# RWKV stage of a two-layer trunk: the state products in one PSUM bank, the other bank for the centred values and the first of each pair of chunk products, and new places for all pieces

## The chip, the core and the metric

One core of a Trainium2 chip runs the whole program. Its engines are named PE (TensorE), ACT (ScalarE), DVE (VectorE), POOL (GpSimd) and SP (SyncE, which issues the DMAs). The metric is the device time of one launch in microseconds (us).

## The reference, cut to what matters

Two layers on 2048 tokens of width 1024, each wrapped in RMS norms. Layer 0 is gated linear attention, layer 1 is RWKV-7 time mixing. The change is in the second one, whose recurrence per head is:

```python
p = h @ w_in
p = p + mu * (token_shift(p) - p)
r, k, v, gate, wd, ad = jnp.split(p, [...])
...
def step(S, inp):
    r_t, w_t, k_t, v_t, kk_t, a_t = inp
    sa = jnp.einsum('bhvk,bhk->bhv', S, -kk_t)
    S = (S * w_t[:, :, None, :] + sa[..., None] * (kk_t * a_t)[:, :, None, :]
         + v_t[..., None] * k_t[:, :, None, :])
    y = jnp.einsum('bhvk,bhk->bhv', S, r_t)
    return S, y
...
y = ((y - mean) * lax.rsqrt(var + GN_EPS)).reshape(B, T, RWKV_WIDTH)
...
y = y * jax.nn.silu(gate)
return y.astype(h.dtype) @ w_out
```

## The kernel before

The kernel runs the linear attention first (until about 890 us), then its output projection mixed with the start of the RWKV layer, then 32 RWKV steps (one step is one pair of heads and 512 tokens; `step`), and the last output projection. An RWKV step is cut into about 150 named pieces: a piece is a few instructions of one engine. The table `PLACE` gives every piece a number. Step n puts a piece at time n plus that number, and one heap hands all pieces of all steps out in the order of these times, under a manual schedule for PE, DVE, ACT and POOL. So the table alone decides what stands behind what on each engine, and pieces with numbers 2.x of one step stand between pieces 0.x of the step two later. The projections of the coming step are the filler: a piece `f` or `e` issues six 128x512 matmuls into a bank `ps_pj` (sixteen such pieces in most steps, twenty in each eighth).

PSUM has eight banks, given out by tag: `PB` says how many banks a tag has, and a tile takes the next one of its tag in turn, waiting until the last reader of that bank is done. Before: pj 2, tp 2, x 1, ch 2, y 1.

The pieces that the texts speak of, in the order in which one step needs them:

- `pn`, `n_ln`, `n_exp`, `unit`, `ra_a`, `bk_b`: the key's norm (PE, ACT, ACT, DVE, DVE, DVE).
- `pA` (L1361): products of all chunks, for four chunks at a time, two banks (one for each head); `mask` (DVE, L1370) and `diag` (ACT, L1380, reads the masked tile into `AD`) follow.
- `pB`, `tokens` (ACT, L1397): chunk keys turned. `elim` (28 DVE pieces, L1422 and L1425), `spread` (DVE, L1436 and L1438), `inv_t`, then `pL`, `pM`, `pW`, `pT` (PE, bank x) with `wt`, `Ti`, `Tl` between them (ACT, L1495, L1501, L1516): the triangular inverse.
- `pv` and `ve`: the values times a centring matrix. `pv` fills one bank in two halves, `pv0` and `pv1`, and `ve0` and `ve1` (ACT, L1325, four copies each) read them out, the first half before `pv1` is issued.
- `X` (ACT, L1527 and L1528), `pX` (PE, bank x), `Z` (ACT, L1544), `turn` (PE, L1564), `turned` (ACT, L1568), `pG` (PE), `G` (DVE, L1583): the chunk maps; `pG0` and `pG1` of the texts are the maps of the first and the last four chunks (two pieces each).
- `pS`, `next_state` (ACT, L1604): eight chunk states in a chain, each one matmul and two ACT instructions.
- `py` (bank y), `y_copy` (ACT, L1618), `y_high`, `y_sq` (ACT, L1628, L1623), `y_low` (DVE, L1633), `pg` (PE), `g_ln`, `g_exp` (ACT, L1642, L1646): the output and its norm. `pw` and `pa` are the products of the decay and the rate, `s_exp` (ACT, L1177) reads `pw`.

PE rows have line L103 (the helper `mm`) and are known by their tiles. What the change touches of the allocation:

```python
T.pv = self.ps("tp", [P, NC_ // 2, 2, C])
...
T.pA[cg] = [self.ps("tp", [P, 4, 2 * C]) for _ in range(2)]
...
T.pG[cg] = [self.ps("tp", [P, 4, 2 * C]) for _ in range(2)]
...
T.pS[c] = self.ps("ch", [P, 2, C])
...
T.pg = self.ps("ch", [P, TB])
```

## Time and profile before

| what | value |
|---|---|
| time, median of 3 runs | 2500.66 us (2500.08 to 2507.4) |
| profiled execution: its own time | 2500.48 us |
| profiled execution: span of the trace | 2498.4 us |
| busy PE / weight loads / ACT / DVE / POOL | 2404.0 / 2011.4 / 1646.3 / 1601.1 / 1065.7 us |
| the same, share of the span | 96% / 81% / 66% / 64% / 43% |
| PE idle before its instructions, 1050 to 2300 us, largest | 18.1 us behind `ve` |

A launch takes 2.08 us more than the span of its trace. The busy time of PE is modelled at the ends of its matmuls, so 96% doesn't say how much of it could go; that is read from the idle time ahead of single instructions, which stands in square brackets in a timeline, with what ended it.

### The profile page before, as it was taken

The page shows a single profiled execution, that of the slowest core. Times are in us where ns is not written, and L with a number is a line of the kernel's source. Part 1 is how long each engine was busy: PE and PEld are TensorE (multiplying, and loading weights), DVE is VectorE, ACT ScalarE, POOL GpSimd, SP SyncE. Part 2 cuts the span into 40 slices and gives each one's busy share as a digit, 9 for nine tenths or more (in the row PEclk, how much of TensorE's full clock was granted, in tenths as well). Part 3 has the DMA queues.
Part 4 walks back from the last instruction along what each step waited for, and adds up shares of the span by engine and source line. Part 5 has one row for each costly group of instructions (what it writes and reads, how often), then busy time and mean ns, then how long its engine had stood idle before and what let it go on. Part 6 is the DMA issues. An engine that isn't in the chain of part 4 may idle for free.

```text
span 2498.4 us, 53047 instructions
## 1 busy us (share of the span) xinstructions
PE 2404.0 (96%) x20049; PEld 2011.4 (81%) x20049; DVE 1601.1 (64%) x3339; ACT 1646.3 (66%) x3890; POOL 1065.7 (43%) x1557
## 2 busy tenths in 40 slices
PE   7999999999999998989999999999999999998998
PEld 6988888898878877767878788778788777887777
DVE  6544676346743368887777776777767787776432
ACT  6534565434533356876888988888888889886531
POOL 3213423123456556766543434334343434343442
PEclk9999999999999999998999999999999999999999
DMA  4211333113546565444433333333333333323482
GB/s 148 81 57 51 110 114 104 43 60 95 165 149 223 162 221 176 145 141 138 150 113 132 125 118 114 109 120 125 124 110 114 113 123 123 120 88 111 149 256 93
DMA packets 251863, 312.85 MB, mean 125 GB/s; under 512 B 18746, under 2 KB 180185, under 8 KB 251609
## 3 DMA queue, kind: packets, MB, share of 16 engines
q1 hardware_dynamic: 251608, 309.47, 37.4%
q8 instruction: 159, 2.61, 0.4%
q14 instruction: 96, 0.78, 0.1%
HBM read 230.77 MB, written 78.64 MB: 124 GB/s over the span
## 4 chain that ended last, share of the span: by engine, by line
PE 37%; ACT 18%; DVE 4%; issue 2%; DMA 1%; POOL 1%; POOLq 0%; SPq 0%; ACTq 0%; DVEq 0%
PE ps_pj L103 20%; PE ps_tp L103 9%; PE ps_x L103 3%; ACT AD L1380 2%; PE ps_ch L103 2%; ACT ve L1604 2%; ACT ts L836 1%; ACT ve L1325 1%; PE ps_y L103 1%; ACT BK L1397 1%; ACT y L1618 1%; PE ps_tp L1564 1%; ACT wt L1495 1%; ACT sq L1278 1%; DVE pp L1422 1%
## 5 line engine op out<-in xcount | busy, mean ns | idle before, releaser
L103 PE MATMUL ps_pj<-R,wh 128*128 128x512 f32 x3648 | 1172.8, 402 | 3.8 <-ACT wh L139 1.0
L103 PEld LDWEIGHTS ps_pj<-R,wh 128*128 128x128 f32 x3648 | 656.5, 190 | 131.0 <-issue 3.4
L103 PE MATMUL ps_pj<-R,wl 128*128 128x512 f32 x1824 | 718.2, 394 | 1.1 <-POOL wl L994 1.1
L103 PEld LDWEIGHTS ps_pj<-R,wl 128*128 128x128 f32 x1824 | 343.8, 188 | 79.8 <-POOL wl L994 1.9
L1604 ACT ACTIVATE ve<-ps_ch,cs 64x64 f32<-64x64 f32 x448 | 137.8, 308 | 61.3 <-PE ps_ch L103 52.5
L1422 DVE TENSOR_TENSOR pp<-L 128x14 f32<-128x14 f32 (+6 forms) x448 | 168.1, 375 | 10.5
L103 PE MATMUL ps_tp<-R,wh 128*128 128x512 f32 x512 | 158.3, 390 | 2.1 <-DVE ts L400 1.7
L1425 DVE TENSOR_TENSOR L<-L,pp 128x14 f32<-128x14 f32 (+6 forms) x448 | 139.9, 312 | 12.2
L832 POOL TENSOR_SCALAR carr<-ts 128x1 f32<-128x1 f32 x132 | 34.2, 259 | 241.1 <-ACT ts L836 240.8
L1551 POOL TENSOR_SCALAR A<-ra 64x512 f32<-64x512 f32 x128 | 90.0, 703 | 103.4 <-PE ps_x L103 51.9
L308 POOL TENSOR_TENSOR s<-s,cc 128x1 f32<-128x1 f32 (+1 forms) x96 | 57.6, 602 | 150.7 <-DVE s L306 138.4
L103 PE MATMUL ps_ch<-ve,BK 128*128 128x128 f32 x512 | 109.5, 296 | 7.8 <-ACT ve L1604 7.5
L103 PEld LDWEIGHTS ps_tp<-R,wh 128*128 128x128 f32 x512 | 95.8, 188 | 22.8 <-issue 2.5
L103 PEld LDWEIGHTS ps_ch<-ve,BK 128*128 128x128 f32 x512 | 87.1, 189 | 30.9 <-ACT ve L1604 11.4
L1380 ACT COPY AD<-A 32x128 f32<-32x128 f32 x256 | 105.1, 411 | 10.2 <-DVE A L1370 7.2
L836 ACT ACTIVATE ts<-ps_pj,prm 128x512 f32<-128x512 f32 x132 | 91.4, 692 | 18.7 <-PE ps_pj L103 10.7
L1370 DVE TENSOR_TENSOR A<-ps_tp,mask 128x512 f32<-128x512 f32 x128 | 82.3, 683 | 32.6 <-PE ps_tp L103 32.6
L103 PE MATMUL ps_tp<-R,wl 128*128 128x512 f32 x256 | 99.7, 390 | 0.0
L1583 DVE TENSOR_TENSOR BK<-ps_tp,BK 128x256 f32<-128x256 f32 x128 | 53.7, 419 | 69.6 <-PE ps_tp L103 69.6
L103 PE MATMUL ps_pj<-wh,R 128*128 128x256 f32 (+1 forms) x500 | 94.7, 287 | 0.0
L103 PE MATMUL ps_ch<-wh,R 128*128 128x256 f32 (+1 forms) x500 | 94.3, 286 | 0.0
L798 POOL TENSOR_SCALAR y<-BK,cs 128x256 f32<-128x256 f32 x64 | 36.6, 571 | 132.4 <-DVE BK L800 121.3
(358 smaller groups left out, 5518.3 us busy)
## 6 DMA issues: line engine op xcount, KB each, us to landing
wh<-w SPq DMA_DIRECT2D x99, 512.0 KB
wl<-w SPq DMA_DIRECT2D x99, 512.0 KB
w<-wh SPq DMA_DIRECT2D x33, 512.0 KB
w<-wl SPq DMA_DIRECT2D x33, 512.0 KB
Ti<-in_gla_w_in_dram SPq DMA_DIRECT2D x32, 512.0 KB
ws<-in_gla_w_in_dram SPq DMA_DIRECT2D x32, 512.0 KB
...
```

Source lines behind the costliest of these rows:

```text
L103: return self.nc.tensor.matmul(out, lhsT, rhs, start=start, stop=stop)
L308: nc.gpsimd.tensor_tensor(r[:, 0:w], u[:, 0:w], self.nhalf.broadcast_to([P, w]), op=ALU.pow)
L798: nc.gpsimd.tensor_scalar(Qf[:, n % 2, :], Qn, f[:, n:n + 1], 0.0, op0=ALU.mult, op1=ALU.add)
L832: self.put(name + ".carry", lambda: nc.gpsimd.tensor_scalar(cr, ts[:, TB:TB + 1], 1.0, 0.0, op0=ALU.mult, op1=ALU.add))
L836: nc.scalar.activation(ts[:, 1:TB + 1], pp, AF.Copy, scale=self.v["mu"][:, blk:blk + 1])
L1370: dve.tensor_mul(T.A[cg][:, :, :, h, :], V(T.pA[cg][h]), V(self.mask.unsqueeze(1).broadcast_to([P, 4, 2 * C])))
L1380: act.copy(T.AD[q, :, :, cg * 4:cg * 4 + 4].rearrange("p t u c -> p c u t"), T.A[cg][q, :, 0, h, 32 * b:32 * b + 32].rearrange("p c (u t) ...
L1422: dve.tensor_mul(T.u, T.M[:, s + 1:16, s:s + 1].broadcast_to([P, m, s]), T.M[:, s:s + 1, 0:s].broadcast_to([P, m, s]))
L1425: dve.tensor_add(T.M[:, s + 1:16, 0:s], T.M[:, s + 1:16, 0:s], T.u)
L1551: pool.tensor_scalar(T.A[cg][H[h], :, :, h, :], T.ra[H[h], cg * 4:cg * 4 + 4, :].rearrange("p c (b t) -> p c b t", b=2), 1.0, 0.0, op0=ALU ...
L1583: dve.tensor_add(o, T.pG[cg][h][:, :, x], o)
L1604: act.activation(o, x, AF.Copy, scale=k)
```

## The change

The tag ch goes from two banks to one, and a new tag tv gets the bank. In the linear attention and in the output projections the two tiles that took ch in turn now name ch and tv, one each. In an RWKV step `pS` and `pg` share the one bank ch; `pv` moves from tp to tv; of each pair of `pA` and of `pG` the first moves to tv and the second stays in tp. All numbers of `PLACE` are new (two lines of the table are shown).

```diff
-    PB = dict(pj=2, tp=2, x=1, ch=2, y=1)
+    PB = dict(pj=2, tp=2, x=1, ch=1, tv=1, y=1)
...
-                tp = self.ps("ch", [P, 4, P])
+                tp = self.ps(("ch", "tv")[ch], [P, 4, P])
...
-            pv = [self.ps(t, [P, w]) for t in ("ch", "ch", "pj", "pj")]
+            pv = [self.ps(t, [P, w]) for t in ("ch", "tv", "pj", "pj")]
...
-        ("pick", (0.773633, 0.800002)), ("pn", 0.286577), ("pv", (0.805045, 0.854518)), ("pw", 0.000000),
...
+        ("pick", (0.737006, 0.854736)), ("pn", 0.283275), ("pv", (0.740546, 0.872544)), ("pw", 0.000000),
...
-                T.pv = self.ps("tp", [P, NC_ // 2, 2, C])
+                T.pv = self.ps("tv", [P, NC_ // 2, 2, C])
...
-                T.pA[cg] = [self.ps("tp", [P, 4, 2 * C]) for _ in range(2)]
+                T.pA[cg] = [self.ps(t, [P, 4, 2 * C]) for t in ("tv", "tp")]
...
-                T.pG[cg] = [self.ps("tp", [P, 4, 2 * C]) for _ in range(2)]
+                T.pG[cg] = [self.ps(t, [P, 4, 2 * C]) for t in ("tv", "tp")]
```

Outside the RWKV steps the order of PE's rows is the same as before, only the banks' names differ. Inside, three places matter.

The first is PE around the second half of `pv`. `cen,vx` are the two halves of `pv`, `kkx,bo` and `s,bo` are the bonus (`pb`), `wt,TT` is `pT`. Before:

```order
L103 MATMUL ps_tp_17338<-kkx_17249,bo 128x512
L103 MATMUL ps_tp_17338<-s_17258,bo 128x512
L103 MATMUL ps_tp_17354<-cen,vx_16513 128x128 x2
L103 MATMUL ps_pj_17279<-R_9711,wh_17104 128x512
...
L103 MATMUL ps_pj_17279<-R_9711,wl_17105 128x512
L103 MATMUL ps_x_17374<-wt_17345,TT_17203 32x32 x16
L103 MATMUL ps_tp_17354<-cen,vx_16513 128x128 x2
```

Now:

```order
L103 MATMUL ps_tv_17321<-cen,vx_16500 128x128 x2
L103 MATMUL ps_pj_17276<-R_9719,wh_17092 128x512
...
L103 MATMUL ps_pj_17276<-R_9719,wl_17093 128x512
L103 MATMUL ps_tp_17354<-kkx_17207,bo 128x512
L103 MATMUL ps_tp_17354<-s_17277,bo 128x512
L103 MATMUL ps_x_17357<-wt_17337,TT_17189 32x32 x16
L103 MATMUL ps_tv_17321<-cen,vx_16500 128x128 x2
```

Between the two halves stand twelve projection matmuls instead of six, and the bonus too. Further on, the stretch from `pX0` (`sq,Ti`) to `pG0` (`sq,A`) before:

```order
L103 MATMUL ps_tp_17447<-xw_13746,uh 128x512
L103 MATMUL ps_tp_17447<-xw_13746,ul_9162 128x512
L103 MATMUL ps_x_17451<-sq_17156,Ti_9165 128x128 x4
L1564 MATMUL ps_tp_17456<-ident,A_16542 128x128 x4
L1564 MATMUL ps_tp_17464<-ident,A_16543 128x128 x4
L103 MATMUL ps_x_17471<-a_17348,Ti_9165 128x128 x4
L103 MATMUL ps_tp_17486<-sq_17156,A_16542 128x128
L103 MATMUL ps_tp_17487<-sq_17156,A_16542 128x128
```

Now, from the last projection matmul behind `pv1`:

```order
L103 MATMUL ps_pj_17276<-R_9719,wl_17093 128x512
L103 MATMUL ps_x_17420<-sq_17193,Ti_9165 128x128 x4
L103 MATMUL ps_tp_17433<-xw_13766,uh 128x512
L103 MATMUL ps_tp_17433<-xw_13766,ul_9162 128x512
L1564 MATMUL ps_tp_17438<-ident,A_16552 128x128 x4
...
L1564 MATMUL ps_tp_17461<-ident,A_16553 128x128 x4
L103 MATMUL ps_tv_17467<-sq_17193,A_16552 128x128
L103 MATMUL ps_tp_17468<-sq_17193,A_16552 128x128
L103 MATMUL ps_tv_17467<-sq_17193,A_16552 128x128
...
L103 MATMUL ps_x_17478<-a_17344,Ti_9165 128x128 x4
```

`pX0` now follows `pv1` after six projection matmuls (twelve and `pw` before); six stand between the two `turn`; `pX1` (`a,Ti`) has moved behind `pG0`. The third place is ACT behind the last norm product `pg`. Before, with `g_ln` on L1642:

```order
L1527 COPY sq_19565<-BK_19123 64x4x64
L1528 COPY sq_19565<-A_18938 64x4x64
L1527 COPY sq_19565<-BK_19123 64x4x64
L1528 COPY sq_19565<-A_18938 64x4x64
L1642 ACTIVATE ce_19519<-ps_ch_19553,cc 128x512
L1646 ACTIVATE ce_19519<-ce_19519 128x512
L1380 COPY AD_19622<-A_19541 32x4x2x16 x2
```

Now, and the rows around `ve0` (L1325):

```order
L1642 ACTIVATE ce_19518<-ps_ch_19538,cc 128x512
L1646 ACTIVATE ce_19518<-ce_19518 128x512
L1527 COPY sq_19602<-BK_19155 64x4x64
...
L1380 COPY AD_19618<-A_19552 32x4x2x16 x2
L180 CAST R_19270<-qs_19549 128x512
L1663 ACTIVATE ce_19518<-ce_19518,cc 128x512
...
L836 ACTIVATE ts_19678<-ps_pj_19503,prm 128x512
L1325 COPY ve_19785<-ps_tv_19731 64x2x64 x4
L1527 COPY a_19755<-BK_19156 64x4x64
```

The four copies X0 stood ahead of `g_ln` and stand behind it now; from `g_ln` to `ve0` ACT's work is otherwise the same set in another order. The cast on L180 (a piece of the next quarter's input) is there in some steps only, before as now.

On PE the piece `pA` of the first four chunks moves from ahead of `pg` to behind it, twelve projection matmuls instead of eighteen stand between `py` of the last four chunks and `pg`, and six more stand ahead of that `py`.

## Rows read from the trace of the kernel before

**Rows 1.** The page's first part: busy us, share of the span, instructions.

```profile
PE 2404.0 (96%) x20049; PEld 2011.4 (81%) x20049; DVE 1601.1 (64%) x3339; ACT 1646.3 (66%) x3890; POOL 1065.7 (43%) x1557
```

**Rows 2.** Waits on PE, 1050 to 2300 us: total us, times, longest.

```profile
PE ps_tp L103 <- ACT ve L1325: 18.1, 21, 1.2
PE ps_tp L103 <- DVE A L1583: 10.1, 4, 2.9
PE ps_y L103 <- ACT y L1618: 6.1, 25, 0.3
```

**Rows 3.** Timeline of DVE, `scan` of two steps: start us, us, instruction.

```profile
1268.15 1.23 DVE L1190 TENSOR_TENSOR_SCAN ce<-m,s 128x520 f32<-128x520 bf16 x1
...
2212.59 1.23 DVE L1190 TENSOR_TENSOR_SCAN ce<-m,s 128x520 f32<-128x520 bf16 x1
```

**Rows 4.** Timeline of PE over one step, 1516 to 1560 us.

```profile
1516.74 1.16 PE L103 MATMUL ps_tp<-sq,A 64*128 64x128 f32 x16
...
1532.86 1.16 PE L103 MATMUL ps_y<-A,ve 128*128 128x128 f32 x8 [0.24 <-ACT y L1618]
...
1538.07 1.16 PE L103 MATMUL ps_tp<-ra,bk 64*128 64x128 f32 x16
1539.16 0.50 PE L103 MATMUL ps_ch<-sq,bo 128*128 128x512 f32 x1
1539.50 0.39 PE L103 MATMUL ps_ch<-a,bo 128*128 128x512 f32 x1
...
1552.14 0.71 PE L103 MATMUL ps_tp<-cen,vx 128*128 128x128 f32 x4 [0.82 <-ACT ve L1325]
1552.61 0.70 PE L103 MATMUL ps_pj<-R,wh 128*128 128x512 f32 x2
...
1555.43 0.40 PE L103 MATMUL ps_tp<-xw,uh 128*128 128x512 f32 x1
...
1555.90 1.06 PE L103 MATMUL ps_x<-sq,Ti 128*128 128x128 f32 x8
1556.80 1.04 PE L1564 MATMUL ps_tp<-ident,A 128*128 128x128 f32 x8
1557.67 1.12 PE L103 MATMUL ps_x<-a,Ti 128*128 128x128 f32 x8
1558.72 1.16 PE L103 MATMUL ps_tp<-sq,A 64*128 64x128 f32 x16
```

**Rows 5.** Timeline of ACT, the same step, 1532 to 1562 us.

```profile
1539.70 0.41 ACT L1527 COPY sq<-BK 64x256 f32<-64x256 f32 x1 [2.35 <-PE ps_ch L103]
...
1552.11 0.40 ACT L1501 COPY Ti<-TD 32x256 f32<-32x256 f32 x1
1552.53 0.63 ACT L1667 ACTIVATE ce<-ce 128x512 f32<-128x512 f32 x1
...
1555.09 1.07 ACT L1325 COPY ve<-ps_tp 64x128 f32<-64x128 f32 x4
1556.19 0.69 ACT L1177 ACTIVATE s<-ps_tp,neg 128x512 f32<-128x512 f32 x1
1556.99 0.59 ACT L1544 COPY sq<-ps_x 128x512 f32<-128x512 f32 x1
1557.49 1.08 ACT L1568 COPY A<-ps_tp 128x512 f32<-128x512 f32 x2
```

**Rows 6.** ACT by shape, 1354 to 1396.6 us: count, busy us, mean ns, idle before.

```profile
L180 ACT CAST R<-qs 128x512 fp32r<-128x512 f32 x2 | 1.2, 621 | 0.0
```

**Rows 7.** Timeline of DVE, one `spread` and `y_low`.

```profile
1528.80 1.42 DVE L1436 TENSOR_SCALAR L<-L,m 128x128 f32<-128x128 f32 x1
...
1536.02 0.69 DVE L1633 TENSOR_TENSOR a<-ce,sq 128x512 fp32r<-128x512 f32 x1 [1.06 <-ACT ce L1623]
```

**Rows 8.** Timelines of DVE and POOL in an early step, 1067 to 1075 us.

```profile
1069.68 2.44 DVE L1425 TENSOR_TENSOR L<-L,pp 128x50 f32<-128x50 f32 x1
...
1069.67 2.38 POOL L994 TENSOR_TENSOR wl<-ws,wh 128x1024 fp32r<-128x1024 f32 x1
```

More of the change, by code (lines that the diff above doesn't have):

```diff
@@ L1115 @@
-        ("ra_a", 0.360648), ("ra_r", 0.372763), ("rx.carry", 0.000000), ("rx.high", 0.050128), ("rx.low", 0.008916),
-        ("rx.mu", 0.036595), ("rx.sum", 0.006546), ("s_exp", 0.000000), ("s_inv", 0.078332), ("s_ln", 0.021706),
-        ("scan", 0.130101), ("sg.carry", 0.003165), ("sg.high", 0.119746), ("sg.low", 0.007345), ("sg.mu", 0.021216),
-        ("sg.sum", 0.072091), ("sg_exp", 2.750405), ("sg_inv", 2.852664), ("sg_ln", 2.782531), ("sg_mul", 2.933067),
-        ("spread", (1.288641, 1.397433, 1.481477, 1.503470)), ("state", 1.083019), ("swap", 0.001655),
@@ L1120 @@
-        ("tanh1", 0.020633), ("tanh2", 0.143899), ("tanh3", 0.011919), ("tanh4", 0.142745),
-        ("tokens", (0.750451, 0.758029)), ("turn", (2.007162, 2.011537)), ("turned", (2.011747, 2.020252)),
-        ("unit", 0.345054), ("unit_diag", 0.875903), ("up", (0.231461, 0.676446, 0.750351)),
-        ("ve", (0.823375, 0.989609)), ("vx.carry", 0.016566), ("vx.high", 0.000000), ("vx.low", 0.121784),
-        ("vx.mu", 0.108162), ("vx.sum", 0.000000), ("wa.carry", 0.000000), ("wa.high", 0.208304),
@@ L1125 @@
-        ("wa.low", 1.581877), ("wa.mu", 0.060487), ("wa.sum", 0.040044), ("wt", (1.795746, 1.796796)),
-        ("y_bonus", 2.750505), ("y_copy", (2.355033, 2.451301)), ("y_gate", 3.027929), ("y_high", 2.475990),
-        ("y_low", 2.512093), ("y_norm", 2.690675), ("y_sq", 2.488221), ("zero", 0.000000),
+        ("G", (2.057791, 2.058873, 2.254885, 2.254985)), ("Ti", (1.929397, 1.883744, 1.720077, 1.821047)),
+        ("Tl", (1.889433, 1.901516)), ("X", (1.626971, 1.649089, 1.804681, 1.843655)), ("Z", (1.981484, 2.064862)),
@@ new lines @@
+        ("ends", 0.479514), ("eye", (2.040937, 1.839415, 2.066864, 2.037152)),
+        ("f", (0.230560, 0.009982, 0.032014, 0.772622, 0.321701, 0.934046, 0.501021, 0.348374, 0.483928, 0.516599,
+          0.577397, 0.202052, 0.742654, 0.214999, 0.710276, 1.263188)),
+        ("face", 0.111527), ("g_exp", 2.617785), ("g_ln", 2.587725), ("high", 0.105059), ("inv_add", 1.691159),
+        ("inv_t", 1.567000), ("inv_tt", 1.613016), ("inv_tt2", 1.745944), ("k_mul", 0.267358), ("k_rate", 0.253999),
@@ new lines @@
+        ("kk", 0.024419), ("kk_high", 0.059252), ("kk_low", 0.200493), ("kk_sq", 0.130018), ("kx.carry", 0.086284),
+        ("kx.high", 0.111167), ("kx.low", 0.000000), ("kx.mu", 0.034267), ("kx.sum", 0.029304), ("lanes", 0.731905),
+        ("low", 0.000000), ("low16", 1.648917), ("mask", (0.583854, 0.665698, 0.668432, 0.675897)),
+        ("n_exp", 0.316493), ("n_ln", 0.291725),
+        ("next_state", (2.106521, 2.186252, 2.255661, 2.271972, 2.293186, 2.359124, 2.443100, 3.028979)),
+        ("out.high", 0.069957), ("out.low", 0.064583), ("pA", (0.583654, 0.583754, 0.640310, 0.661127)),
[5 rows of a table added]
@@ new lines @@
+        ("py", (2.285831, 2.484813)), ("r_high", 0.651447), ("r_low", 0.710870), ("r_mul", 0.528444),
+        ("ra_a", 0.364273), ("ra_r", 0.402070), ("rx.carry", 0.000000), ("rx.high", 0.030431), ("rx.low", 0.098494),
+        ("rx.mu", 0.051553), ("rx.sum", 0.000000), ("s_exp", 0.000000), ("s_inv", 0.034824), ("s_ln", 0.022155),
+        ("scan", 0.118487), ("sg.carry", 0.044015), ("sg.high", 0.196236), ("sg.low", 0.000000), ("sg.mu", 0.029164),
+        ("sg.sum", 0.121349), ("sg_exp", 2.698384), ("sg_inv", 2.938921), ("sg_ln", 2.714790), ("sg_mul", 2.940456),
@@ new lines @@
+        ("spread", (1.485457, 1.512426, 1.512526, 1.517589)), ("state", 1.382171), ("swap", 0.058982),
+        ("tanh1", 0.003213), ("tanh2", 0.170327), ("tanh3", 0.007827), ("tanh4", 0.133594),
+        ("tokens", (0.789636, 0.817519)), ("turn", (2.004669, 2.012633)), ("turned", (2.013256, 2.014701)),
+        ("unit", 0.322667), ("unit_diag", 1.333155), ("up", (0.648137, 0.698798, 0.980181)),
+        ("ve", (0.842861, 1.008529)), ("vx.carry", 0.001457), ("vx.high", 0.078141), ("vx.low", 0.069351),
@@ L1128 @@
+        ("vx.mu", 0.116796), ("vx.sum", 0.079648), ("wa.carry", 0.003483), ("wa.high", 0.709989),
+        ("wa.low", 0.879892), ("wa.mu", 0.076285), ("wa.sum", 0.020004), ("wt", (1.780001, 1.787818)),
+        ("y_bonus", 2.707933), ("y_copy", (2.383638, 2.498877)), ("y_gate", 3.073780), ("y_high", 2.506883),
+        ("y_low", 2.516923), ("y_norm", 2.624351), ("y_sq", 2.504460), ("zero", 0.000000),
     )
```

28 lines of the change are left out of this document (7 added, 21 removed), and 8 rows, old and new, of the table PLACE.

## The prediction

> **What bounds the kernel now.** The page's first part comes first: PE is busy 96% of the span, ACT 66%, DVE 64% [rows 1]. So PE sets the time, and a change of order can only win what PE idles, or lose by new idling. The waits on PE say where it idles in the RWKV steps: 18.1 us behind `ve` in 21 places, 10.1 us behind `G` in only 4, 6.1 us behind `y_copy` in 25 [rows 2]. The two large regular ones recur in nearly every step; the 10.1 us belong to a few early and late steps. For the length of a step I take one instruction that each step has once, DVE's `scan`: 22 steps from 1268.15 to 2212.59, 944.4 us [rows 3]. Two of them hold four more filler pieces, so 24 more matmuls each; a filler matmul costs 0.235 us (twelve from 1552.61 to 1555.43 [rows 4]), so these are 11.3 us, and a plain step is on average 42.4 us. Then the timeline of one step, `pG0` to `pG0`, 1516.74 to 1558.72, 41.98 us [rows 4]: PE waits twice, 0.82 us at `pv1` and 0.24 us at the second `py`. Without them the step would take 40.9 us: that is the floor, as long as the filler and the products stay what they are.
>
> **The change part by part.** No instruction is added or removed, the banks stay eight, and outside the RWKV steps PE's order is the same. So linear attention, the output projections and the DMA count at nothing: there the two banks were taken in turn and still are.
>
> *The states' single bank.* `pS` of a chunk reads the state that `next_state` of the chunk before writes from PSUM, so the chain was serial with two banks as well. What one bank adds is between steps: the first `pS` of a step needs the last `next_state` of the step before, which ACT now issues behind both `turned` and one more instruction, some 2 us behind `turned0` (each of its kind takes 0.5 to 0.7 us [rows 5]), while PE has `pG0`, `pX1`, six filler and `pa` before that `pS`, 4.0 us [rows 4]; and the last `pS` needs `g_ln`, which follows `pg` by 0.8 us, while that `pS` comes five matmul groups later. I count both at nothing. If the cover were gone, it would cost at most the two ACT instructions of one `next_state` (about 0.6 us) in each step.
> The Trainium skill's PSUM — Partial Sum Buffer, section on PSUM bank collisions, says to guard PSUM by bank and quadrant and not by address. It speaks against putting more into one bank. The trace agrees: `pv1` writes the half of its bank that `ve0` doesn't read, and still starts at 1552.14, when `ve0`'s copies have ended and ACT's next instruction starts at 1552.11 [rows 4, 5]. The sum below holds the wait either way.
>
> *`pv1`.* I measure from the start p of `pg`. Before, PE would have reached `pv1` at 1552.14 - 0.82 - 1539.16 = 12.16 us after p [rows 4]. Now `pA0` (1.09 us, 1538.07 to 1539.16) lies behind `pg`, the number of filler runs on the way is the same (four pieces), so PE arrives at 13.0 to 13.25; the lower value counts that two fewer changes from filler to small tiles occur. ACT: `ve0` ends when the chain from `g_ln` has run. Its instructions are those that took from 1539.70 to 1552.11 before, 12.4 us without a gap [rows 5], in another order; it starts when the second `pg` matmul ends, at 1539.89, plus 0.04, so at p + 0.77. `ve0` ends at p + 13.2. The wait of 0.82 us falls to 0.0 to 0.2 us; I take 0.15.
>
> *`pX0`.* PE needs 1555.90 - 1552.14 = 3.76 us from `pv1` to `pX0` before; now six filler matmuls (1.41) and `pw` (0.47) less, 1.88. It arrives at 13.2 + 1.88 = p + 15.1. `pX0` needs all pieces of `Ti` and `Tl`; ACT does them right behind `ve0` and two X copies. Before, this stretch took 1552.11 to 1555.09, 2.98 us with one 0.64 us instruction (1552.53) that now stands behind it [rows 5]: 2.34, so p + 15.5. New wait 0.4 us.
>
> *`pG0`.* From `pX0` PE does `pX0` and `pw` (0.9 + 0.47), `turn0` (0.44), six filler (1.41 and 0.05 for the change), `turn1` (0.43): 3.7 us [rows 4]. ACT needs `pX0`'s end (1.06), then `Z0` 0.59, `s_exp` 0.69, `ve1` 1.08, half of `turned` 0.54 [rows 4, 5] and a few hand-overs: 4.05. New wait 0.35 us. At `pG1` `Z1` comes nearly with PE; 0.1 us.
>
> *Second `py`.* Six more filler matmuls (1.4 us) stand ahead of it, and the `y_copy` that it waited 0.24 us for is issued ahead of the last `next_state` but one. Wait gone.
>
> *`pg`.* From the second `py` to `pg` was 1539.16 - 1532.86 = 6.30 us; `pA0` (1.09) and six filler (1.41) leave: 3.80, and `pg`'s second matmul 0.34 later, 4.14. It needs `y_low`, which started 1536.02 - 1532.86 = 3.16 us after the second `py` (one copy and both squares on ACT lie between, as they do now) and takes 0.69: 3.85 [rows 4, 7]. It fits with 0.29 us to spare.
>
> Sum for a step without the L180 cast: waits 0.15 + 0.4 + 0.35 + 0.1 = 1.0 us instead of 1.06, and two changes from filler to small tiles saved. Those have no row of their own here; each is between nothing and one filler slot (0.235 [rows 4]), I take 0.1, so 0.2 together: 41.7 us against 41.98. Where the cast (0.62 us, [rows 6]) is in the chain, both kernels pay; before this made the plain average 42.4, now I take 42.0 to 42.1. Gain 0.25 to 0.4 us a step, over 22 steps about 7 us.
>
> *Early and late steps.* In four steps `pG1` waited 10.1 us for `G` [rows 2], because one DVE `elim` took 2.44 us while POOL subtracted weights for 2.38 us [rows 8]. POOL now runs that pair behind three more pieces, and PE has 3 us of other work (`pX1`, filler, `pa`, `pS`) instead of 1.4 before `pG1` needs the bank. I count half of it won, 5 us, since the block of DVE remains and hits another piece; bounds 0 and 10, and up to 4 lost elsewhere in the other six steps.
> The Trainium skill's SBUF — State Buffer, Who interferes with whom, says that a DVE instruction with two SBUF inputs and a POOL instruction that reads SBUF exclude each other for the whole instruction. The two rows agree (2.44 beside 2.38 us).
>
> Total: -7 - 5 = -12 us on the profiled execution's 2500.48 us, which stands 0.18 under the median: 2488.5 us.
>
> **The rivals.**
> *Waits only move (no change).* ACT is the engine that sets `ve0`, `Ti` and `turned`, and its chain from `pg` to `pG0` has no gap to give. If ACT is 0.3 us a step later than worked out (one more cast in the chain, 0.62, in half of the steps), the regular gain is gone, and what the early steps win is lost there: 2494 to 2503, about 2499. For it: the three new waits are small differences of sums of ten rows. Against it: each sum is made of rows that had no gap.
> *PE at its floor.* If PE's arrival is later by 0.4 us at these places, the waits are covered: 1.06 us times 29 steps and 8 us early, 2460 to 2470. Against it: `ve1` and `s_exp` lie ahead of `turned`.
> *Slower: `pg` waits for `y_low`.* The margin is 0.29 us. All four `spread` now stand right around `y_low`, and one such instruction took 1.42 us, twice the 0.69 of `y_low`, which has four times its elements [rows 7]. If DVE comes to `y_low` late, every us is PE's, and ACT's chain from `g_ln` shifts with it: at 1 us late, 0.7 us in 30 steps less the 0.25 gained, +14 us, 2514. It decides from 0.5 us late. Against it: DVE idled 1.06 us before `y_low` [rows 7], and `pn`, which starts DVE's row of pieces, now has 2.4 us more before the second `py`.
>
> **How the numbers follow.** My forecast (2480 to 2494) gets 0.56, no change 0.24, the floor 0.07, slower by `y_low` or by a wait that I did not see 0.13. What a measurement of this kernel tells from no change is 0.3%, 7.5 us: under 2493.2 is faster, over 2508.2 slower. Nearly nine tenths of the forecast, the floor, and little of the second case lie under the first: 0.57; slower most of the last case: 0.11; the rest 0.32. The range leaves out the floor and the worst of the slower case: 2474 to 2505.
>
> **What would show it.** Right: waits on PE behind `ve` fall under 6 us; new rows of PE waiting for `Ti` at ps_x and for `turned` at the first `pG`; none for `y_copy`; a plain step of 41.7 to 42.1 us; the 2.9 us waits for `G` gone or halved. Wrong: PE waiting for `y_low` at ps_ch, or for `next_state` at ps_ch in a place where it did not before, or early steps as long as ever.

## The result, and the profile after

The changed kernel takes 2441.57 us (median of 4, 2436.67 to 2446.07) beside 2504.03 (4 runs of the kernel before): ratio 0.9763, 95% interval 0.9742 to 0.9785. By the medians it is 62 us faster, by the ratio 59, where 12 were forecast; the time lies under the range, and under the rival with PE at its floor too. The span of its profiled execution is 2444.3 us, 54.1 less than before. That execution is the slowest of the four (2446.07), while the profiled one of the kernel before (2500.48) is near the fastest of its four, so the profiles show less than the medians.

The page's first part after the change, which answers to [rows 1]:

```profile
PE 2373.1 (97%) x20049; PEld 1995.9 (82%) x20049; DVE 1532.4 (63%) x3339; ACT 1651.3 (68%) x3890; POOL 1058.2 (43%) x1557
```

The waits on PE after, 1000 to 2250 us (total us, times, longest), which answer to [rows 2]:

```profile
PE ps_tv L103 <- ACT A L1568: 6.4, 26, 0.3
PE ps_x L103 <- POOL A L1551: 5.4, 23, 0.3
PE ps_tv L103 <- ACT ve L1325: 3.0, 6, 0.9
...
PE ps_ch L103 <- DVE BK L1583: 2.4, 2, 1.6
PE ps_ch L103 <- DVE a L1633: 0.9, 1, 0.9
```

The wait at `pv1` is gone from the regular steps, two small ones stand at `pG0` (behind `turned`, L1568) and `pX0`, none at the second `py`, and the waits for `G` (L1583) fall from 10.1 us to 2.4. The releaser named at `pX0` is POOL's `alpha`, which `pX0` doesn't read; what came last there is ACT's `Ti`, which ends at 1483.40, 0.10 us ahead of `pX0`, as two timelines of one step after the change show, which answer to [rows 4, 5]. PE's (start us, us, instruction, idle before):

```profile
1467.94 0.40 PE L103 MATMUL ps_ch<-sq,bo 128*128 128x512 f32 x1
...
1481.19 0.71 PE L103 MATMUL ps_tv<-cen,vx 128*128 128x128 f32 x4
...
1483.50 1.13 PE L103 MATMUL ps_x<-sq,Ti 128*128 128x128 f32 x8 [0.20 <-POOL A L1551]
...
1487.61 0.37 PE L103 MATMUL ps_tv<-sq,A 64*128 64x128 f32 x1 [0.25 <-ACT A L1568]
```

ACT's, the same step:

```profile
1480.00 1.07 ACT L1325 COPY ve<-ps_tv 64x128 f32<-64x128 f32 x4
...
1483.00 0.40 ACT L1501 COPY Ti<-TD 32x256 f32<-32x256 f32 x1
1483.31 0.62 ACT L1667 ACTIVATE ce<-ce 128x512 f32<-128x512 f32 x1
1484.67 0.59 ACT L1544 COPY sq<-ps_x 128x512 f32<-128x512 f32 x1 [0.73 <-PE ps_x L103]
1485.15 0.70 ACT L1177 ACTIVATE s<-ps_tp,neg 128x512 f32<-128x512 f32 x1
1485.87 1.08 ACT L1325 COPY ve<-ps_tv 64x128 f32<-64x128 f32 x4
1486.97 1.07 ACT L1568 COPY A<-ps_tp 128x512 f32<-128x512 f32 x2
```

A step is best cut in two: from `pg` to the first `pG`, and from there to the next `pg`. Windows of such a step of the kernel before (us, busy time and count of PE, PEld, DVE, ACT, POOL; then the granted clock, DMA share, GB/s):

```profile
1497.16:1516.74 19.58, 18.75 (x302) 15.53 (x300) 12.19 (x29) 18.41 (x46) 9.34 (x18) 1.00 0.31 104
1516.74:1539.16 22.42, 22.18 (x144) 18.29 (x143) 17.44 (x40) 17.32 (x40) 7.86 (x15) 1.00 0.32 117
```

And of the changed kernel:

```profile
1467.94:1487.61 19.67, 19.13 (x309) 15.17 (x308) 13.56 (x32) 18.39 (x47) 10.84 (x21) 1.00 0.20 67
1487.61:1509.09 21.48, 21.48 (x134) 18.40 (x135) 13.75 (x38) 17.50 (x40) 5.83 (x11) 1.00 0.44 155
```

The first half keeps its length; the second, in which PE is busy all the time, is 0.94 us shorter. From `pg` to `pg` a plain step without the cast takes 41.15 us (42.00 before, 19.58 + 22.42), one with it 41.17 (42.43 before), 41.7 in four. In those four the cast starts 7.2 us behind `pg`, early in ACT's chain. In the others it starts 15.9 us behind it, in the gap that ACT has ahead of `Z0`, and the gap falls from 0.73 to 0.22 us (ACT, the step whose `pg` starts at 1344.41):

```profile
1360.34 0.60 ACT L180 CAST R<-qs 128x512 fp32r<-128x512 f32 x1
1361.17 0.59 ACT L1544 COPY sq<-ps_x 128x512 f32<-128x512 f32 x1 [0.22 <-PE ps_x L103]
```

Where the 54 us of span went, by the starts of `pg`: the first `pg` of the RWKV layer comes 6.6 us earlier (from 889 us on 732 matmuls stand ahead of it instead of 750), steps 1 to 6 take 16.2 less (262.6 beside 278.8), the 22 steps behind them 24.4 less (919.1 beside 943.4), and the last steps with the final projection make up the other 7.

### The profile page after: what moved, and what is told of

Read it like the earlier page. It is cut to its first block, busy times and chain, and to the rows that moved or that the text cites. A ratio compares the mean times of both kernels' runs of the same rounds, so it can differ in the third digit from the quotient of the medians.

```text
span 2444.3 us, 52899 instructions
## 1 busy us (share of the span) xinstructions
PE 2373.1 (97%) x20049; PEld 1995.9 (82%) x20049; DVE 1532.4 (63%) x3339; ACT 1651.3 (68%) x3890; POOL 1058.2 (43%) x1557
## 5 line engine op out<-in xcount | busy, mean ns | idle before, releaser
L1422 DVE TENSOR_TENSOR pp<-L 128x14 f32<-128x14 f32 (+6 forms) x448 | 136.1, 304 | 11.0
L1425 DVE TENSOR_TENSOR L<-L,pp 128x14 f32<-128x14 f32 (+6 forms) x448 | 131.9, 294 | 8.1
L1551 POOL TENSOR_SCALAR A<-ra 64x512 f32<-64x512 f32 x128 | 79.8, 624 | 58.3 <-issue 34.2
L1583 DVE TENSOR_TENSOR BK<-ps_tv,BK 128x256 f32<-128x256 f32 x64 | 26.9, 421 | 123.3 <-PE ps_tp L103 109.3
L994 POOL TENSOR_TENSOR wl<-ws,wh 128x1024 fp32r<-128x1024 f32 x36 | 86.8, 2412 | 1.5
L139 ACT CAST wh<-ws 128x512 fp32r<-128x512 f32 (+2 forms) x74 | 40.9, 602 | 68.7 <-PE ps_pj L103 68.6
```

The lines of the kernel that those rows point to most:

```text
L139: self.nc.scalar.copy(hi[:, c], src[:, c])
L994: nc.gpsimd.tensor_sub(lo, st, hi.bitcast(F32))
L1422: dve.tensor_mul(T.u, T.M[:, s + 1:16, s:s + 1].broadcast_to([P, m, s]), T.M[:, s:s + 1, 0:s].broadcast_to([P, m, s]))
L1425: dve.tensor_add(T.M[:, s + 1:16, 0:s], T.M[:, s + 1:16, 0:s], T.u)
L1551: pool.tensor_scalar(T.A[cg][H[h], :, :, h, :], T.ra[H[h], cg * 4:cg * 4 + 4, :].rearrange("p c (b t) -> p c b t", b=2), 1.0, 0.0, op0=ALU ...
```

## The experiments

Each is the kernel named with a small edit; ratios are against runs of the kernel before beside it. Its median lies between 2496 and 2504 us from one set of runs to the next, so two experiments are best compared by their ratios. "Half" means the halves of a step above.

### Banks and order

**The banks alone.** The changed kernel with the table PLACE of the kernel before.

```diff
+    PB = dict(pj=2, tp=2, x=1, ch=1, tv=1, y=1)     # and the tags that go with it
     PLACE = _places(                                # as before
```

> The changed kernel's banks (one for the states' products, the other for the centred values and the first of each pair) with every place of the kernel before. Theory (the gain is in the places): in the kernel before the last next_state of a step ends at 1520.32 and the first pS of the next step starts at 1520.56, so one bank costs that pS nothing as long as both keep their places; pv1 still waits for ve0, since both are halves of one bank whichever it is: about 2500 us, 2492 to 2508, and still some 17 us of PE's waits behind ve. Rival (the banks themselves free the order): a large part of the 62 us comes back, 2440 to 2475, and the waits behind ve fall under 6 us. Second rival (one bank for the states makes pS wait at the seam between steps, hidden in the changed kernel by its places): 0.5 to 1 us in each of 31 steps, 2515 to 2535.

2505.68 us, 1.0018 (1.0004 to 1.0032): no gain. Plain steps 42.0 and 42.4 as before; 20.3 us of waits behind `ve`. In three steps, one in each eight, PE waits 1.8 us for the state: the waits of PE from 1050 to 2300 us have a row that before lacked, since one bank holds a step's first `pS` until ACT has read the last one's:

```profile
PE ps_ch L103 <- ACT S L1604: 5.3, 3, 1.8
```

The three waits are of one length, 1.76 us, but the steps are not (the first two of them, windows from `pg` to `pg`):

```profile
1241.35:1286.90 45.55, 42.39 (x448) 33.79 (x446) 32.05 (x75) 37.76 (x88) 19.91 (x35) 1.00 0.33 112
1587.29:1634.41 47.12, 44.12 (x448) 34.82 (x446) 31.43 (x75) 37.76 (x88) 16.54 (x32) 0.96 0.28 97
```

Before, they took 43.96 and 43.92. At full clock the wait costs 1.6 us; with a stretch at a granted clock of 0.50 behind it, in the second step and the third, it costs 3.2 and 3.1: the same 448 matmuls keep PE busy 1.7 us longer.

So the gain is in the places.

**The wait at `pv1`, covered.** One place in the kernel before: `pv1` behind six filler matmuls.

```diff
-        ("pv", (0.805045, 0.854518))
+        ("pv", (0.805045, 0.98))
```

> The kernel before with one place changed: the second pv stands behind six filler matmuls (1.41 us) that it stood ahead of, so ve0 has ended when PE comes to it; banks, pairs and all else as before. Theory (the regular gain of 1.1 us a step is mostly PE's wait at pv1, which any cover of 0.8 us takes away, with the next need, pX0, then just met: before, pX0 started 0.81 us after ACT had ended what it needs): 0.6 to 0.8 us in some 27 steps, 2479 to 2487 us, waits behind ve under 4 us and new ones of at most 0.2 us at pX0. Rival (waits only move, since ACT's chain sets the step): 2494 to 2504, with 0.4 us and more at pX0 or pG0 in each step.

2499.0 us, 0.9994 (0.998 to 1.0008). The theory fell. The waits behind `ve` went from 18.1 us to none, and the halves of the step hardly moved:

```profile
1495.82:1515.22 19.40, 19.22 (x303) 15.46 (x301) 12.20 (x29) 18.35 (x46) 9.15 (x18) 1.00 0.35 120
1515.22:1537.66 22.44, 22.17 (x143) 18.24 (x142) 17.45 (x40) 17.38 (x40) 8.06 (x15) 1.00 0.29 105
```

PE idles 0.18 us instead of 0.83 in the first half, but the half is only 0.18 us shorter: `pX0` now starts 0.41 us behind the last matmul of `pw`, where matmuls of that shape follow each other in 0.23, and in eight steps with the cast in this half PE waits 0.7 us there, 5.3 in all. ACT works through that half without a gap (18.4 of 19.4 us busy, hand-overs between), so it lasts as long as ACT's chain, wherever PE waits in it. That gave the next theory: what counts in full is what PE does in the second half, or can move from it into the first half's wait.

**The second `py` behind filler.** In the kernel before, where it waits for `y_copy` [rows 4].

```diff
-        ("py", (2.262737, 2.401556)), ("y_copy", (2.355033, 2.451301)), ("y_high", 2.475990)
+        ("py", (2.262737, 2.4788)), ("y_copy", (2.355033, 2.4800)), ("y_high", 2.4805)
```

> The kernel before with the second py (and the two ACT copies behind it, in their old order) moved behind the six filler matmuls that followed it. Theory of two halves (a step's stretch from pg to the first pG lasts as long as ACT's chain, so filler put ahead of pv1 there won nothing; the stretch from the first pG to pg is PE's alone, and what PE idles or spends there counts in full): the second py starts 0.63 us after the pS before it, where after a filler it would take 0.23, so 0.35 to 0.5 us in 27 steps or so, 2485 to 2492 us, with the stretch from the first pG to pg 22.0 instead of 22.4 us and no wait behind y_copy. Rival (waits only move everywhere in the step): 2496 to 2504, with PE waiting for y_low at pg instead.

2489.71 us, 0.996 (0.9948 to 0.9973), as the theory said. The move has a price that comes once: in the last step `pg` waits 4.5 us for `y_low`. Windows of a step, the second half at 21.91 instead of 22.42:

```profile
1499.75:1519.42 19.67, 18.98 (x302) 15.63 (x300) 13.23 (x31) 18.49 (x46) 9.87 (x20) 1.00 0.30 103
1519.42:1541.33 21.91, 21.91 (x143) 18.19 (x142) 16.39 (x39) 17.32 (x40) 7.00 (x14) 1.00 0.34 121
```

**`pA0` behind `pg`.** In the kernel before.

```diff
-        ("pA", (0.531789, 0.544892, 0.587574, 0.606821))
+        ("pA", (0.5552, 0.5553, 0.587574, 0.606821))
```

> The kernel before with the first pair of chunk products (pA0, 1.09 us of small matmuls) moved from ahead of pg to behind it: the one step of the changed order that shortens PE's half and fills the wait in ACT's half, in the old banks. Theory of two halves: the stretch from the first pG to pg falls from 22.4 to about 21.2 us, and the one from pg to the first pG, 19.6 us with a wait of 0.8 us at pv1, takes the 1.1 us in mostly in place of that wait: 0.6 to 1.0 us in 28 steps, 2473 to 2485 us, and the waits behind ve under 6 us. Rival (the banks and pairs are needed for it; or the chunk maps, which start from pA0, come later on DVE and ACT and move the end of ACT's chain with them): 2492 to 2506, with the second stretch longer by what the first lost.

2482.27 us, 0.9924 (0.9905 to 0.9942). The 1.1 us leave PE's half, and nearly two thirds of them disappear in ACT's (windows of a step):

```profile
1496.15:1516.18 20.03, 19.95 (x318) 16.31 (x316) 13.20 (x31) 18.49 (x46) 9.76 (x20) 1.00 0.35 124
1516.18:1537.42 21.24, 21.00 (x128) 17.50 (x127) 16.64 (x39) 17.32 (x40) 7.27 (x14) 1.00 0.28 102
```

**Both.** The two edits above together.

> The kernel before with both moves at once: the second py behind six filler matmuls (alone: stretch from the first pG to pg 22.42 to 21.92 us) and the first pair of chunk products behind pg (alone: that stretch 21.24, the other 19.57 to 20.03). Theory of two halves: they add up, since both shorten PE's half: 20.7 to 20.8 us there, 20.0 to 20.4 in the other, a plain step of 40.8 us without a cast and 41.2 with one, so the whole regular gain of the changed kernel (41.15) in the old banks: 2464 to 2474 us. Rival (pg then comes 3.7 us after the second py, and waits for y_low, which needs 3.85): PE's half stays at 21.2 or more, 2476 to 2486 us, with a wait behind L1633 in each step.

2477.69 us, 0.9916 (0.989 to 0.9943). Windows of a step with the cast:

```profile
1365.32:1385.79 20.47, 20.25 (x318) 16.28 (x316) 15.74 (x30) 19.60 (x49) 10.35 (x21) 1.00 0.37 126
1385.79:1406.55 20.76, 20.76 (x128) 17.45 (x127) 17.16 (x43) 17.18 (x40) 6.41 (x11) 1.00 0.35 128
```

The halves add up as forecast; the 22 steps behind the sixth take 920.0 us, the changed kernel's 919.1, the kernel before's 943.4. **The whole regular gain can be had by two moves in PE's order, in the old banks.** The time as a whole is 4 us above the forecast and inside the rival's range, but in the regular steps the rival's wait isn't there; `pg` waits for `y_low` in five early steps, 6.2 us, and 4.4 us in the last. The first six steps are nearly as long as before (276.5 us beside 278.8), and one late step waits for `G` (45.5 us).

### Early steps

**The weight pieces' places.** The kernel before with the changed places of POOL's pairs `wh`, `wl`, and of the cast and its difference (all `*.high` and `*.low`); then without `part.*`, the cast; then the reverse: the changed kernel with the old ones.

```diff
-        ("kx.high", 0.033900), ("part.high", 0.172155), ("part.low", 0.000000), ("wa.low", 1.581877)
...
+        ("kx.high", 0.111167), ("part.high", 0.132292), ("part.low", 0.076132), ("wa.low", 0.879892)
```

> The kernel before with the changed kernel's places for the weight pieces alone (the POOL pairs that make wh and wl, and the ACT cast and DVE difference of the next activations). Theory (in the early steps POOL's subtraction of a weight blocks one DVE instruction that PE's G waits for, and the changed kernel moved the pair away from it): of the 16 us that the first six steps lost less in the changed kernel, 8 to 16 come here too, 2484 to 2494 us, and the waits of PE behind G fall from 10.1 us to under 4. Rival (the early steps win by the order of the other pieces, or by the granted clock that follows from it): 2496 to 2506, waits behind G as before or moved elsewhere.

> The kernel before with the changed kernel's places for POOL's pairs wh and wl alone; the ACT cast and its DVE difference keep the old places (in the run with both, the second to fourth step took 44.0 us instead of 47.4 to 51.0, with no stretch at half clock, and the steps with a cast 43.0 instead of 42.4). Theory (POOL's pairs make the long waits for G in the early steps, and the halved clock that follows each; the cast's place makes the regular loss): the early gain of 12 to 14 us stays, the cast steps are back at 42.4 to 42.6, 2483 to 2490 us. Rival (the cast's place made the early gain, or the early gain is lost in the last steps): early steps of 47 us and more again, or 2495 to 2503.

> The changed kernel with the weight pieces' places of the kernel before (the counterpart of the one above). Theory: the early steps lose 8 to 16 us again, 2450 to 2458 us, with waits of 2 us and more behind DVE in four or five of the first six steps; and if the cast of 0.62 us on ACT is hidden in the changed kernel by where it stands, the steps with it take 0.3 to 0.6 us more than those without, another 5 to 9 us. Rival (the order of the other pieces does it): 2438 to 2446, plain steps 41.2 with and without the cast.

The first: 2499.21 us, 0.9991 (0.9979 to 1.0003). No gain in all, but steps 2 to 4 take 14.2 us less, 132.0 beside 146.2, and the profiles show two terms of it, idle time and the clock. In the kernel before `pG1` waits 2.87 us, and behind that wait PE runs at a granted clock of 0.50, 1.2 of its 2.4 GHz. Its timeline there:

```profile
1123.84 2.71 PE L103 MATMUL ps_tp<-a,A 64*128 64x128 f32 x16 [2.87 <-DVE A L1583]
...
1127.91 0.63 PE L103 MATMUL ps_pj<-R,wl 128*128 128x512 f32 x1
1128.34 1.05 PE L103 MATMUL ps_pj<-R,wh 128*128 128x512 f32 x2
```

Its windows, over the three stretches at half clock in these steps and over the three steps:

```profile
1076.20:1079.60 3.40, 3.40 (x10) 2.72 (x10) 3.23 (x10) 0.62 (x2) 0.00 (x0) 0.50 0.94 289
1124.00:1130.80 6.80, 6.78 (x27) 5.52 (x27) 4.77 (x17) 0.64 (x3) 0.46 (x2) 0.50 0.81 256
1171.80:1178.60 6.80, 6.74 (x27) 5.43 (x27) 4.78 (x16) 0.70 (x3) 0.52 (x2) 0.50 0.49 156
...
1048.60:1194.80 146.20, 133.43 (x1328) 108.40 (x1326) 115.81 (x210) 109.32 (x258) 98.13 (x121) 0.94 0.42 142
```

The same `pG1` with the new pieces, and then the window of the three steps:

```profile
1118.02 0.46 PE L103 MATMUL ps_tp<-a,A 64*128 64x128 f32 x2 [0.44 <-DVE A L1583]
1118.69 1.13 PE L103 MATMUL ps_tp<-a,A 64*128 64x128 f32 x14 [0.21 <-DVE L L1425]
```

```profile
1050.70:1182.70 132.00, 124.93 (x1328) 101.95 (x1326) 115.95 (x211) 109.31 (x258) 97.16 (x120) 1.00 0.46 158
```

PE idles 7.1 us instead of 12.8 (146.20 - 133.43), and is busy 8.5 us less with the same 1328 matmuls, as a clock of 0.94 instead of 1.00 makes it (0.06 of 146.2 is 8.8). So the long waits cost about twice themselves: three of 2.2 to 2.9 us, 7.9 in all, and the 8.5 of slower work behind them. The Trainium skill's TensorE: Matmul & The Clock Gate, section Terms, puts the penalty at the time spent at the reduced clock times the share that is missing; the three stretches at 0.50, 17.0 us in all, give 8.5 us by it, and the trace agrees. What was won there goes only in part where the profile shows it. The eight steps with a cast behind the first `pG` take 43.0 to 43.3 us instead of 42.4 to 42.7, 4.8 us in all. Ahead of the first `pg` the filler now waits 10.2 us for POOL's `wl` (1.1 before), while other waits there are gone, so that this `pg` comes 1.2 us later (waits on PE, 890 to 1010 us):

```profile
PE ps_pj L103 <- POOL wl L994: 10.2, 3, 5.4
```

The profiled execution, at 2494.52 us, is also the lowest of the ten; the rest of what went isn't shown.

The second, without the cast's places: 2499.78 us, 0.9999 (0.9988 to 1.001). The cast steps are back at 42.4 to 42.6, as said, so the cast's place made that loss; steps 3 and 4 stay short (43.8), but step 2 waits 3.8 us for `G` and takes 48.5, and a late step 47.8. So POOL's pairs alone give 10.1 of the 14.2 us in steps 2 to 4 (136.1), and what they give goes ahead of the first `pg`, which comes 6.9 us later (the filler waits 10.8 us for `wl` there), and in the late step: the time is the rival's.

The third: 2450.95 us, 0.9797 (0.9775 to 0.982), by the medians some 9 us above the changed kernel, though the two intervals overlap. Eight more steps with a cast take 41.7 us instead of 41.17, which is 4 us of it; the early steps lose nothing (130.4 us for steps 2 to 4, clock 1.00). The time lies in the theory's range, but by luck: the larger of its two losses didn't come. The changed kernel itself runs these steps no faster, and has two short stretches at half clock in them:

```profile
1042.90:1174.20 131.30, 125.37 (x1328) 102.90 (x1326) 109.43 (x212) 109.49 (x259) 97.58 (x120) 0.97 0.48 163
```

So the changed kernel hides the cast by its place, and something else protects its early steps too.

**What protects them.** DVE's block isn't gone. In the changed kernel's second step an `elim` still takes 2.46 us beside POOL's pair, ahead of the first `G`, where one of the same shape takes 0.22 in a regular step; PE then waits 1.64 us instead of 2.88 (DVE, POOL, PE):

```profile
1064.16 2.46 DVE L1425 TENSOR_TENSOR L<-L,pp 128x54 f32<-128x54 f32 x1
1064.14 2.40 POOL L994 TENSOR_TENSOR wl<-ws,wh 128x1024 fp32r<-128x1024 f32 x1
1068.38 0.46 PE L103 MATMUL ps_ch<-ve,BK 128*128 128x128 f32 x2 [1.64 <-DVE BK L1583]
```

Three attempts follow. First `pG1` of the kernel before behind the first `pS` and six filler matmuls:

```diff
-        ("G", (2.044193, 2.050266, 2.091647, 2.158500)), ("pG", (2.042512, 2.043850, 2.078154, 2.078254))
+        ("G", (2.044193, 2.050266, 2.1010, 2.158500)), ("pG", (2.042512, 2.043850, 2.1000, 2.1001))
```

> The kernel before with the second pair of chunk maps (pG1, which waited 10.1 us for G in four early and late steps) behind the first pS and six more filler matmuls, 1.5 us of cover; the weight pieces stay where they were. Theory (the early loss is the wait for G and the stretch at half clock that follows it, and any cover for G takes both): waits behind G from 10.1 to under 5 us, the second to fourth step from 47.4 to 51.0 us each to 44 to 46, in all 6 to 12 us, 2487 to 2494 us, and plain steps as before within 0.1. Rival (the halved clock comes whatever PE waits, or the wait goes to pS or py): 2495 to 2505, steps of 47 us and more, stretches at half clock as before.

2535.64 us, 1.0145 (1.0115 to 1.0175): slower by more than either theory. The first `pS` needs the same `G` and waits 3.1 us itself; and `pa`, which now follows `pG1` at once, needs a bank of tp that `pG1` holds until DVE has read it, in nearly every step (waits on PE, 1050 to 2300 us; the releaser named is DVE's instruction behind `G`):

```profile
PE ps_tp L103 <- DVE L L1425: 26.3, 28, 1.0
...
PE ps_ch L103 <- DVE BK L1583: 10.4, 4, 3.1
```

Then the changed kernel with the old pieces and `pX1` back ahead of the first `pG`, so that `G` has less cover, and the kernel before with DVE's `y_gate` behind the first `G` instead of ahead of it:

```diff
-        ("pX", (1.980924, 2.017199))
+        ("pX", (1.980924, 2.0130))
...
-        ("y_gate", 3.027929)
+        ("y_gate", 3.0600)
```

> The changed kernel with the weight pieces' old places, as in the run of that name, and with pX1 moved back ahead of the first pG, so that G has 0.92 us less cover before the first pS and pG1 need it. Theory (pX1 and pa are the cover that keeps the early steps short): waits of 1.5 to 2.5 us behind G (L1583) return at the first pS of two or three early steps, with stretches at half clock, and the second to fourth step take 45 to 48 us instead of 42.1 to 44.6: 2454 to 2464 us. Rival (the early steps are protected by something else): early steps as in that run, 2446 to 2453.

> The kernel before with DVE's y_gate alone moved from ahead of the first two G to behind them; it took 0.74 us (0.66 to the next start) right ahead of G in the early step where pG1 waited 2.9 us. Theory (DVE's row ahead of G makes the early waits, and a wait of some 2 us or more is followed by a stretch at half clock): the waits of 2.9 us fall to 2.2 to 2.4 and most stretches at half clock stay, 2493 to 2499 us. Rival (y_gate was the whole difference): waits under 1.5 us, no half clock, 2484 to 2490.

The one: 2443.21 us, 0.9775 (0.9759 to 0.9791), under both ranges: no early loss, 1.3 us the longest wait behind `G`; the cover by `pX1` is not it. The other: 2495.45 us, 0.9978 (0.9964 to 0.9992): the waits of 2.9 us fell to 2.3, as forecast, with half clock behind both; the fourth step, whose wait fell to 1.7 us, had none and took 44.3 us instead of 47.8. So DVE's row ahead of `G` is a part of it, 0.6 us of 2.9; which other place does the rest stays open.

### The parts together

**Sums.** The second `py`, `pA0` and `pG1` moved as above, in the old banks; the first two and all new places of the pieces, in the old banks; and the new banks with old places but for the first two moves, `y_gate`, and these:

```diff
-        ("pa", 0.155239), ("pG", (2.042512, 2.043850, 2.078154, 2.078254))
+        ("pa", 0.0770), ("pG", (2.042512, 2.043850, 2.0785, 2.0786))
```

> All three moves together in the old banks: the second py later, the first pair of chunk products behind pg, the second pair of chunk maps later. Theory (the gain lies in the order and the banks only allow it to go a little further): the sum of the parts, 2454 to 2466 us, within 1% of the changed kernel. Rival (without the freed banks the parts undo each other): 2472 or more.

> The kernel before, in its old banks, with the second py later, the first pair of chunk products behind pg, and the changed kernel's places for the weight pieces and the cast. Theory (regular and early gain have separate causes and add up): the regular 23 us remain but for 0.3 to 0.5 us in the steps with a cast, and the second to fourth step come to 42 to 44 us without half clock, 10 us or more: 2460 to 2470 us; what is left to the changed kernel, some 20 to 25 us, lies in the cast steps, the start and the end. Rival (the two hinder each other): 2474 or more.

> The changed kernel's banks with the places of the kernel before but for these: second py later, first pair of chunk products behind pg, pa ahead of the first pS, pG1 behind that pS without filler between, y_gate behind the first G. The weight pieces stay in their old places. Theory: regular steps as in the old banks with the first two moves (23 us won), and the early waits for G fall by pa (0.47 us) and y_gate (0.66) to under 2 us, so that at least half of the stretches at half clock go: 2455 to 2467 us. Rival (the early steps need the pieces' new places or the whole new order): 2470 to 2480, early steps of 46 us and more as before.

2505.83 us, 1.0032 (1.0019 to 1.0045): the wait of `pa` takes back what the two moves won. 2461.75 us, 0.9852 (0.9833 to 0.9872): regular and early gain add up in the old banks; the 22 steps take 918 us and steps 2 to 4 130.7, both as in the changed kernel. What is left, 0.9% by the ratios, lies in the profiles ahead of the first `pg`, which comes 9 us later than in the changed kernel (the filler waits 9.8 us for `wl` there, and PE has 13.6 us at half clock, the changed kernel none), and in the last steps. 2505.04 us, 1.0019 (1.0009 to 1.0029): the rival came nearer, but for a reason that neither named, the price of one bank: the first `pS` waits for the last `next_state` of the step before. The changed kernel's table has that piece earlier (3.029 instead of 3.117); that this is what pays the price there is argued, since no run moved it alone. Its waits on PE, 1050 to 2300 us:

```profile
PE ps_ch L103 <- ACT S L1604: 16.5, 26, 2.4
```

### Beyond the changed kernel

**ACT's half shortened.** In the changed kernel ACT's `ve1` ahead of `Z0`, where ACT idles 0.73 us (row of 1484.67 above), and `sg_inv` later; then also `pw` ahead of `pX0`; `pX1` back ahead of the first `pG`, alone and with these.

```diff
-        ("ve", (0.842861, 1.008529)), ("sg_inv", 2.938921), ("sg_mul", 2.940456)
+        ("ve", (0.842861, 0.9389)), ("sg_inv", 3.005), ("sg_mul", 3.03)
...
-        ("pX", (1.980924, 2.017199)), ("Z", (1.981484, 2.064862))
+        ("pX", (2.0001, 2.0130)), ("Z", (2.0002, 2.064862))
```

> The changed kernel with ve1 on ACT ahead of Z0 (in the place where sg_inv stood, where ACT idled 0.73 us before Z0), and sg_inv with its product behind s_exp. The changed kernel's first pG waits 0.25 us in 26 steps for turned0, which ACT has behind Z0, s_exp and ve1. Theory (this stretch, from pg to the first pG, is set by ACT, so what leaves ACT's chain ahead of turned0 comes back): 0.15 to 0.25 us a step, 2434 to 2439 us beside the changed kernel's 2441.6, with the waits of PE behind L1568 under 2 us. Rival (the wait moves: sg_inv now delays turned0 or ve1 delays Z0): 2440 to 2446, with the same 6 us at pG0 or more at pX0 and turn.

> The changed kernel with ve1 on ACT ahead of Z0, as in the run of that name, and on PE pw ahead of the first pX, which waits 0.21 us in 23 steps for the last piece of Ti: pw's 0.47 us stand in that wait, s_exp then comes ahead of Z0 on ACT. Theory of two halves: pX0's wait goes, and one change from filler to a small tile is saved; Z0 is 0.5 us later, which pG0, 3 us later, doesn't notice: the stretch from pg to the first pG 19.1 to 19.2 instead of 19.39 us, 2429 to 2434 us. Rival (ACT's chain sets this stretch, so the wait goes on to turn or pG0): 2435 to 2440, with a new wait of 0.2 us and more at pG0.

> The changed kernel with pX1 alone moved back ahead of the first pG; the weight pieces keep their new places. Theory of two halves: 0.92 us of PE work goes from PE's half (21.48 to 20.6 us) into the half where PE waits 0.46 us for ACT (19.68 to 20.3), where it fills the wait of 0.25 at pG0: 0.2 to 0.3 us a step shorter in the regular steps; early steps with the new pieces lose at most 3 us: 2434 to 2442 us beside 2441.6. Rival (the cover is needed with the new pieces too): early waits behind G of 2 us again, 2445 to 2455.

> The changed kernel with ve1 on ACT ahead of Z0 and pw ahead of the first pX, as in the run of that name (2429.2 us), and pX1 back ahead of the first pG. Theory of two halves: PE's half falls from 21.5 to 20.6 us, the other rises from 19.0 to 19.4 to 19.8 to 20.1, since its last wait, 0.3 us at pG0 in some steps, is filled: a plain step of 40.4 to 40.6 us instead of 40.5 to 40.8: 2424 to 2430 us. Rival (a fully filled half has no more wait to fill, and G loses its cover): 2430 to 2440.

2437.09 us, 0.9747 (0.9732 to 0.9761): plain step 40.97, no wait at `pG0` left. 2429.2 us, 0.9724 (0.97 to 0.9749): 40.5 to 40.8, 41.0 in four. 2435.15 us, 0.9742 (0.9728 to 0.9757): 40.96, `pX1` moved 0.8 us from one half to the other and filled 0.2 of wait. 2428.23 us, 0.9713 (0.9697 to 0.9729): the fastest, and the only one of the four whose interval is clear of the changed kernel's (0.9742 to 0.9785); from the second it isn't told apart. In the profiles the regular gain is the smaller part in the first and the third: the 22 steps take 916.4, 911.2, 915.0 and 911.3 us (919.1 in the changed kernel), the first six 254.7, 256.6, 253.4 and 253.1 (262.6). Steps 2 to 4 have no stretch at half clock in any of the four and take 124 to 125 us instead of 131; no run shows which place does that. Windows of a step with the cast, with PE busy in both halves:

```profile
1335.74:1355.54 19.80, 19.71 (x318) 16.18 (x316) 15.48 (x34) 19.25 (x49) 9.32 (x18) 1.00 0.30 96
1355.54:1376.33 20.79, 20.71 (x127) 17.57 (x127) 13.67 (x38) 17.62 (x40) 7.68 (x15) 1.00 0.44 161
```

## Why the prediction was wrong

The direction and the places were right: waits behind `ve` at 3.0 us, new waits at `pX0` and `pG0` in the regular steps, none at the second `py`, and one of 0.9 us for `y_low`, at the first `pg`. The slower rival was nearer than that looks (DVE's `y_low` and the second matmul of `pg` on PE, at the end of the step shown):

```profile
1508.54 0.69 DVE L1633 TENSOR_TENSOR a<-ce,sq 128x512 fp32r<-128x512 f32 x1 [2.60 <-ACT sq L1628]
1509.32 0.46 PE L103 MATMUL ps_ch<-a,bo 128*128 128x512 f32 x1
```

DVE is not late behind `spread`, as that rival had it: it idles 2.60 us ahead of `y_low`, for ACT's square. But `y_low` ends at 1509.23, 0.09 us ahead of the matmul that reads it, and where PE does wait for it, at the first `pg`, that distance is 0.05. So 0.04 us were to spare, not 0.29; with the old places of the pieces PE waited there 13 times, 4.7 us in all. The bank of the states cost nothing in the changed kernel; with every old place it cost 5.3 us of waits, with `next_state` in its old place and PE's order moved 16.5. Three terms of the sum were mis-sized.

**The new waits.** Forecast 0.15 + 0.4 + 0.35 + 0.1 = 1.0 us in a step; measured 0 at `pv1`, 0.20 at `pX0`, 0.25 at `pG0`, 0 at `pG1`. ACT's side was right: `ve0` ends at p + 13.13 (1481.07 - 1467.94, forecast 13.2), `pX0` starts at p + 15.56 (forecast 15.5 for `Ti`). PE came later than taken: at `pv1` at p + 13.25, the upper end of 13.0 to 13.25 of which the lower was used, and at `pX0` at 15.36 instead of 15.1. With 40.7 us of PE's own work, which the forecast had right, a plain step is 41.15 instead of 41.7 us.

**The cast.** The prediction let both kernels pay for it and added 0.3 to 0.4 us to the average step. The changed kernel pays only in the four steps where the cast stands early in ACT's chain; in the others it fills ACT's gap ahead of `Z0`, which the prediction didn't look for. With the old places of the pieces eight more steps take 41.7. These two terms are the regular miss, 24 us instead of 7.

**The early and late steps.** Forecast -5, bounds 10 won to 4 lost; the span shows -30 outside the 22 steps. The step that failed is "I count half of it won": it priced the 10.1 us of waits alone and put PE's clock behind them at nothing. The waits themselves stayed inside its bounds (2.4 us are left, so 7.7 won). But steps 2 to 4 ran 17 us at half clock behind the waits, which cost 8.5 us more; a window over [rows 8] with its granted clock would have shown it. The windows show the same ahead of the first `pg` (clock 0.97 before, 1.00 after) and in the first late step (0.96 and 1.00). Between 890 and 2400 us the kernel before has 30.7 us at half clock and the changed kernel 10.2; at half of each that is 10 of the 30 us, an estimate from these stretches. The term also left out that a step outside the 22 gains what a regular one does, 1.1 us (24.4 over 22): another 10 us over nine or ten of them, by the same kind of estimate. That POOL's pair and DVE's `elim` cause the early waits, as [rows 8] suggested, is shown only in part: moving the pieces shortens the waits, but the changed kernel has short ones with the old pieces too, and the block still stands in it.

The rival of moving waits was right about the kernel before (covering `pv1` alone won nothing) and wrong about the change, since `pA0` left the other half. The prediction took the step as one chain with a floor of 40.9 us. It is two halves: in the one that PE fills all that PE saves counts, while in the one that ACT sets PE's work is free until it fills the wait. Nor was 40.9 the floor: with `pw` ahead of `pX0` and `pX1` back, most plain steps take 40.5 to 40.6.
